# Up-projection products held in source order, with two grouped pairs at the start of each second half

## The chip, the cores and the metric

The kernel runs on one core of one Trainium2 chip. The metric is the device time of one execution in microseconds. The kernel before takes 2371.57 us (median of three runs, 2370.21 to 2375.67). Besides, one execution was taken by the hardware profiler; every time inside the kernel in this document is from that trace, in microseconds from the first instruction.

The engines have short names. PE is the matrix engine (its weight loads are listed apart, as PEld), DVE the vector engine, ACT the scalar engine, POOL the general one, and SP issues most of the transfers. A matrix product takes a stationary operand of 128 x 128 and streams up to 512 columns past it. Its results are added up in a bank of PSUM.

## The reference

The program is an encoder of two layers on 256 tokens of width 2048. Each layer has a normalisation, a token mixer (mLSTM in layer 0, HGRN2 in layer 1), a second normalisation, and a gated MLP with a convolution of width 3. The change touches the MLP alone:

```python
D_MODEL, SEQ, DEPTH, D_FF, CONV_W = 2048, 256, 2, 5504, 3

def conv_glu(hn, w_up, conv_w, conv_b, w_down):
    u = hn @ w_up
    a, v = jnp.split(u, 2, axis=-1)
    s = a.shape[1]
    pad = CONV_W // 2
    ap = jnp.pad(a, ((0, 0), (pad, pad), (0, 0)))
    c = conv_b
    for j in range(CONV_W):
        c = c + ap[:, j:j + s] * conv_w[j]
    return (jax.nn.gelu(c, approximate=False) * v) @ w_down

for layer in range(DEPTH):
    ...
    h = h + mix
    h = h + conv_glu(rmsnorm(h, norm_ffn_g[layer]), ffn_w_up[layer], ffn_conv_w[layer],
                     ffn_conv_b[layer], ffn_w_down[layer])
return rmsnorm(h, final_g)
```

Everything is float32. The kernel gets that precision out of products of a reduced kind of float32: each operand is split into a high part and a low part, and high x high, high x low and low x high are added up.

## The kernel before

**Chunks.** All products with weights are cut into chunks (`Chunk`, L124), which `stream` (L324) takes one after the other. A chunk of the kind "fm" has 256 weight columns. Its result is 2 x 128 columns by 256 tokens, in two banks of PSUM, one for each `f`. The chunk runs over `nk` = 16 slices of the input, called tiles here; a slice is 128 of the 2048 features. For every tile and each of the two `f` there are two products. The wide one (L356) has the high part of 128 weight columns stationary (`wh`) and streams 512 columns: the input's high part for 256 tokens and its low part for the same tokens. The narrow one (L360) has the low part stationary (`wl`) and streams the 256 columns of the input's high part. One wide and one narrow product are called a pair here; a chunk has 32 pairs.

**The order in the source.** For each piece of weights `stream` makes a list `ops` of (tile, f, part), with "h" for wide and "l" for narrow (L347). So the products come in turn: wide, narrow, wide, narrow. An entry `i` in `swap` exchanges the narrow product of pair `i` and the wide one of pair `i` + 1 (L348 to L351). This makes wide, wide, narrow, narrow out of these two pairs, and that is called a group here.

**The order on the chip** is not that of the source. The whole program is handed to a scheduler (L1363) that plays it through with estimated times. On each engine it issues, of what its plan has ready, what comes first in the source. Something the plan expects late is overtaken by what stands behind it. Afterwards the order on each engine is fixed, and at run time an engine waits where an input isn't there yet. `pin` (L130) is a call that ties an instruction behind the last one that the source has on the same engine, in issue order alone. It is used for the loads of weights that are `paced` (`late`, L393), and in the first chunk of all.

**The weights' way.** The loads (L394, L135) bring 2048 columns at a time into three buffers, `raw`. ACT makes the high part of 1024 columns (L147), and DVE subtracts it for the low part (L148). There are four buffers for each part, and a piece is made three pieces ahead of its use (`LOOK`). Four tiles of an up chunk fit one piece.

**The MLP** (`ffn`, L1174). The 5504 features are 43 chunks, each with 128 columns of `a` and 128 of `v`. They are done in two halves (L1215). The first half (`part` 0) has 22 up chunks (704 pairs) and then the products with `w_down` for these features. The second half (`part` 1) has 21 up chunks (672 pairs) and its `w_down` products. The latter are 512 columns wide throughout (L236, result `pc` or `mm`, stationary `g` or `sx`). Between the products of a first half's chunk 0, PE also has the transposes of the normalisation (L433) and the small products that spread its factors (L457). The slices of the input are made by ACT (L378) and DVE (L379) from these transposes, so the first chunk's last tiles need slices that are made while the chunk runs. `prepare` (L612) loads weights of the down stage early, combines them on DVE (L631) and stores them; `side.tick` counts products to pace such side work.

Up chunks come from L1226 to L1229. The only groups that the source before has in the MLP are one in the second chunk of each first half (`swap=(3,)`: the fourth and fifth pair) and one in the first chunk of each second half (`swap=(2,)`: the two pairs of the second tile). HGRN's "fm" chunks (L1157) have groups as well.

Of the kernel before, what the change touches and what calls it, by code (L numbers as in the profile page):

```python
# [15 lines left out]
P = 128  # L16
T = 256
# [49 lines left out]
def trunk_kernel(ctx, tc, xT, x_d, fg_d, pp_d, cst_d, w_gate, w_first, w_aq, w_ak, w_av, w_ao, w_aout, w_ao2,  # L67
                 w_bq, w_bv, w_bg, w_bout, w_bo2, w_up, w_d0, w_d1, w_d3, out, mscr, tscr):
    nc = tc.nc
    act, dve, pool, pe = nc.scalar, nc.vector, nc.gpsimd, nc.tensor  # L70
# [22 lines left out]
    class Side:  # L93
        def __init__(self):
            self.now, self.jobs = 0.0, []
# [26 lines left out]


    class Chunk:  # L124
        def __init__(self, kind, src, nk, x, done, before=None, last=False, swap=(), first=False, paced=False):
            self.last, self.swap, self.first, self.paced = last, swap, first, paced
            self.kind, self.src, self.nk, self.x, self.done, self.before = kind, src, nk, x, done, before
            self.width = {"fm": 256, "tm": 512, "st": 512}[kind]

    pin = tc.keep_in_program_order  # L130
# [91 lines left out]
    def banks():  # L222
        return [psm.tile([P, 512], F32, tag="mm", name="mm") for _ in range(2)]
# [100 lines left out]
    def stream(chunks):  # L324
        pieces = split_weights(chunks)
        ready = []

        def fetch():
            p = next(pieces, None)
            if p is not None:  # L330
                ready.append(p)

        for _ in range(LOOK):
            fetch()
        for ch in chunks:
            if ch.before:
                ch.before()
            if ch.kind == "st":
                squares_by_seven(ch, fetch, ready)
                continue  # L340
            ps = banks()
            k = 0
            while k < ch.nk:
                fetch()
                wh, wl, n = ready.pop(0)
                if ch.kind == "fm":
                    ops = [(kk, f, part) for kk in range(n) for f in range(2) for part in "hl"]  # L347
                    for i in ch.swap:  # L348
                        i -= 2 * k
                        if 0 <= i < 2 * n - 1:  # L350
                            ops[2 * i + 1:2 * i + 3] = ops[2 * i + 2], ops[2 * i + 1]  # L351
                    for kk, f, part in ops:
                        x = ch.x(k + kk)
                        c = kk * ch.width + f * P
                        if part == "h":
                            pe.matmul(ps[f], wh[:, c:c + P], x, start=k + kk == 0, stop=False)  # L356
                            continue
                        if f:
                            side.tick(0.65)
                        pe.matmul(ps[f][:, 0:T], wl[:, c:c + P], x[:, 0:T], start=False, stop=k + kk == ch.nk - 1)  # L360
                    k += n
                    continue
                for kk in range(n):
                    x = ch.x(k)
                    st, sp = k == 0, k == ch.nk - 1
                    c = slice(kk * 512, (kk + 1) * 512)
                    ops = [(t, i) for t in range(2) for i in range(3)]
                    if ch.first and k in (0, 2):
                        ops.sort(key=lambda o: (0, 2, 1)[o[1]])
                    for t, i in ops:  # L370
                        a, w = ((0, wh), (0, wl), (T, wh))[i]
                        pe.matmul(ps[t], x[:, a + t * P:a + (t + 1) * P], w[:, c], start=st and i == 0, stop=sp and i == 2)  # L372
                    side.tick(1.3)
                    k += 1
            ch.done(ps)
# [236 lines left out]
    def prepare(tiles, todo, first, period, finished, start, ahead):  # L612

        loaded = []

        def load(i):
            if i < len(todo):
                r = tiles(i)
                for j in range(2):
                    start(r[j], todo[i][0][:, j * 1024:(j + 1) * 1024])  # L620
                loaded.append(r)

        yield first
        load(0)
        for i, (_, dst) in enumerate(todo):
            yield period / 2
            if ahead:
                load(i + 1)
            B11, B22, B21, B12 = (loaded[i][j // 2][:, j % 2 * 512:(j % 2 + 1) * 512] for j in range(4))
            for x, y, out in ((B12, B22, B22), (B12, B11, B12), (B11, B22, B11), (B21, B11, B21)):  # L630
                dve.tensor_tensor(out, x, y, ALU.subtract)  # L631
                yield period / 24
            for j in range(2):
                nc.sync.dma_start(dst[:, j * 1024:(j + 1) * 1024], loaded[i][j])
            yield period / 3
            if not ahead:
                load(i + 1)
        finished.append(True)
# [8 lines left out]
    def store(ch, src, u, todo):  # L647
        ch.stored[u] = tscr[turns["t"]]
        turns["t"] += 1
        todo.append((src[:, 2048 * u:2048 * (u + 1)], ch.stored[u]))  # L650
# [523 lines left out]
    def ffn(layer, norm, nxt):  # L1174
# [5 lines left out]
        def begin():  # L1180
            box["mp"] = stack.enter_context(tc.tile_pool(name="ff", bufs=1))
            box["mp"].tile([P, LEAD], F32, name="lead")
            for ch in pairs:
                ch.pool = box["mp"]
            if ending:
                nxt.begin(box["mp"])
# [28 lines left out]
        for part, (f0, nf) in enumerate(((0, FA), (FA, FB))):  # L1215
            GT, SX, todo, finished = [], {}, [], []
            lists.append((todo, finished))

            def prep(todo=todo, finished=finished, nf=nf):
                if not pairs[0].pool:  # L1220
                    begin()
                side.push(prepare(lambda i: [box["mp"].tile([P, 1024], F32, tag=("wh", "wl")[i % 2], bufs=MORE, name="praw")
                                             for _ in range(2)],
                                  todo, 18.0, (nf * 10.4 - 26.0) / len(todo), finished, late, True))

            for i in range(nf):  # L1226
                chunks.append(Chunk("fm", w_up[layer, f0 + i], KT, norm.x, done_up(f0 + i, i, GT, SX, SEVEN[layer][part]),
                                    prep if i == 0 else None,
                                    swap=(2,) if part and i == 0 else (3,) if f0 + i == 1 else (), paced=True))  # L1229
            def two(src, c0, norm, seven, fly, shares, GT=GT, SX=SX, nf=nf):  # L1230
                ch = pair(src, nf, c0, lambda k: GT[k], lambda u: SX[u], norm, seven)
                ch.waits, left = [], [u for u in seven if u not in fly]
                for n, (todo, finished) in zip(shares, [early[layer]] + lists):
                    for u in left[:n]:
                        store(ch, src, u, todo)
                    if n:
                        ch.waits.append(finished)
                    left = left[n:]
                assert not left
                pairs.append(ch)  # L1240
                return ch

            w0, w1 = w_d0[layer][:, f0 * 1024:(f0 + nf) * 1024], w_d3[layer] if part else w_d1[layer]
            seven, fly = SEVEN[layer][part], FLY[2 * layer + part]
            n = len(seven) - len(fly)
            chunks.append(two(w0, 0, nxt if part else None, seven, fly, (0, 0, n) if part else (FIRST, n - FIRST)))
            chunks.append(two(w1, 2, nxt if part and not ending else None, seven, fly, SPLIT[layer] if part else (0, n)))
            if part:
                chunks[-1].last = ending
                if ending:  # L1250
                    chunks[-2].before, chunks[-1].half = nxt.load, nxt.half
                else:
                    chunks[-1].ends = True
# [12 lines left out]
    nf = FinalNorm()  # L1266
    chunks = mlstm(n0, n1)
    c, close0 = ffn(0, n1, n2)
    chunks += c
    c = hgrn(n2, n3)  # L1270
# [5 lines left out]
    c[0].before = swap  # L1276
    chunks += c
    c, close1 = ffn(1, n3, nf)
    chunks += c
    stream(chunks)  # L1280
    close1()

# [98 lines left out]
```

## Time and profile before

| | us |
|---|---|
| median of the runs | 2371.57 |
| profiled execution | 2370.59 |
| its span, first to last instruction | 2368.6 |
| layer 0, up products of the first half | 389.3 to 634.9 |
| layer 0, up products of the second half | 742.7 to 975.6 |
| HGRN mixer of layer 1 with its products | 1106.0 to 1560 |
| layer 1, up products of the first half | 1665.3 to 1910.8 |
| layer 1, up products of the second half | 2015.1 to 2255.6 |

The profile has one page for the whole execution, with the busy time of each engine, and views that are asked for a stretch, a line or an engine: the waits, the timeline, groups by line, and the busy time by stretches. In the timeline, products of the same group that follow each other directly stand in one row, with their count behind the x. The ends of matrix products are modelled, so two of them seem to overlap; what tells the pace is the distance from one start to the next. Operands are named without their number, so a row of L356 doesn't tell its tile or its chunk; these follow from counting.

### The profile page before, as it was taken

To read this page: it belongs to the slowest core of one execution; us is meant where nothing else is said; L and a number is where in the kernel's file an instruction comes from. 1 tells how busy PE (TensorE), PEld (TensorE's weight loads), DVE (VectorE), ACT (ScalarE), POOL (GpSimd) and SP (SyncE) were. 2 spreads that over 40 slices of the span, in tenths; PEclk is the share of its full clock that TensorE was granted. 3 is DMA by queue.
4 is the path that set the end of the run, shared out by engine and by line. 5 is a ranking of instruction groups with operands and counts; after the bars stand their busy time and mean duration, and the time that the engine had idled before them with its cause. 6 is when DMAs were issued, how large, how long until landed. Compare 5 with 4: busy or idle time off the path is not lost. (4 is left out here: it accounts for less than half of the span.)

```text
span 2368.6 us, 38410 instructions
## 1 busy us (share of the span) xinstructions
PE 2358.2 (100%) x14545; PEld 2018.0 (85%) x14545; DVE 1991.6 (84%) x3087; ACT 1469.8 (62%) x2340; POOL 196.7 (8%) x244
## 2 busy tenths in 40 slices
PE   9999999999999999999999999999999999999998
PEld 8888888888888888888888888888888888888887
DVE  7777687888998898897888888778788889888878
ACT  7655456555665555676777677766555566455565
POOL 0100000000000000000232322220000000000000
PEclk9999999999999999999999999999999999999999
DMA  8776656888889888996656665656788888888896
GB/s 302 238 246 244 213 195 208 298 281 295 307 322 331 303 286 294 323 333 231 211 201 226 205 229 198 212 178 221 267 299 301 292 326 324 294 285 292 310 349 221
DMA packets 122266, 632.97 MB, mean 267 GB/s; under 512 B 13776, under 2 KB 14928, under 8 KB 77664
## 3 DMA queue, kind: packets, MB, share of 16 engines
q1 hardware_dynamic: 120384, 626.51, 75.1%
q0 software_dynamic: 1120, 3.21, 0.8%
q8 instruction: 114, 1.87, 0.3%
q10 hardware_dynamic: 576, 0.79, 0.1%
q14 instruction: 72, 0.59, 0.1%
HBM read 562.24 MB, written 68.22 MB: 266 GB/s over the span
## 5 line engine op out<-in xcount | busy, mean ns | idle before, releaser
L356 PE MATMUL mm<-xt,wh 128*128 128x512 f32 x3776 | 1316.6, 395 | 0.0
L148 DVE TENSOR_TENSOR wl<-raw,wh 128x1024 fp32r<-128x1024 f32 (+1 forms) x844 | 1035.0, 1231 | 231.1 <-ACT wh L147 222.2
L147 ACT CAST wh<-raw 128x1024 fp32r<-128x1024 f32 (+1 forms) x844 | 875.7, 1043 | 530.0 <-PE mm L356 325.6
L360 PE MATMUL mm<-xt,wl 128*128 128x256 f32 x3776 | 1045.6, 279 | 0.0
L356 PEld LDWEIGHTS mm<-xt,wh 128*128 128x128 f32 x3776 | 705.7, 188 | 163.1 <-ACT jk L535 0.4
L360 PEld LDWEIGHTS mm<-xt,wl 128*128 128x128 f32 x3776 | 710.0, 188 | 4.8
L372 PE MATMUL mm<-wh,xt 128*128 128x512 f32 x1024 | 324.4, 392 | 1.3 <-ACT wh L147 1.2
L236 PE MATMUL pc<-wh,g 128*128 128x512 f32 (+1 forms) x716 | 243.1, 388 | 0.1
L372 PEld LDWEIGHTS mm<-wh,xt 128*128 128x128 f32 x1024 | 191.1, 188 | 40.8 <-ACT wh L147 1.8
L631 DVE TENSOR_TENSOR praw<-praw 128x512 f32<-128x512 f32 x252 | 174.1, 691 | 35.4 <-DMA praw<-in_w_d 22.3
L372 PE MATMUL mm<-wl,xt 128*128 128x512 f32 x512 | 199.7, 391 | 0.0
L236 PEld LDWEIGHTS pc<-wh,g 128*128 128x128 f32 x716 | 134.1, 188 | 28.4 <-ACT wh L147 0.9
L236 PE MATMUL mm<-wh,sx 128*128 128x512 f32 x432 | 153.4, 389 | 0.0
L148 DVE TENSOR_TENSOR wl<-T,wh 128x1024 fp32r<-128x1024 f32 (+1 forms) x144 | 136.0, 955 | 16.0 <-ACT wh L147 15.6
L147 ACT CAST wh<-T 128x1024 fp32r<-128x1024 f32 (+1 forms) x144 | 118.5, 834 | 48.4 <-DMA T<-tscr 21.7
L236 PE MATMUL pc<-wl,g 128*128 128x512 f32 (+1 forms) x358 | 138.9, 388 | 0.0
L590 POOL TENSOR_TENSOR hm<-hm,u 128x512 f32<-128x512 f32 x10 | 16.0, 1600 | 1222.4 <-DVE u L589 1170.7
L372 PEld LDWEIGHTS mm<-wl,xt 128*128 128x128 f32 x512 | 96.2, 188 | 18.6
L1194 ACT COPY avc<-mm 128x256 f32<-128x256 f32 x172 | 64.1, 373 | 75.5 <-PE mm L360 75.4
L1070 DVE TENSOR_TENSOR QK<-QK,G 128x256 f32<-128x256 f32 x224 | 104.3, 514 | 6.2 <-ACT kq L1049 5.9
L1049 ACT COPY kq<-QK 128x512 f32<-128x512 f32 x112 | 74.5, 669 | 36.9 <-DVE QK L1070 29.1
L236 PEld LDWEIGHTS mm<-wh,sx 128*128 128x128 f32 x432 | 81.0, 188 | 17.2 <-ACT wh L147 0.5
(246 smaller groups left out, 2259.9 us busy)
## 6 DMA issues: line engine op xcount, KB each, us to landing
raw<-in_w_up SPq DMA_DIRECT2D x172, 1024.0 KB, 6.0
tscr<-praw SPq DMA_DIRECT2D x126, 512.0 KB, 6.7
praw<-in_w_d SPq DMA_DIRECT2D x120, 512.0 KB, 6.7
raw<-in_w_bq SPq DMA_DIRECT2D x48, 1024.0 KB, 5.0
T<-tscr SPq DMA_DIRECT2D x63, 768.0 KB, 7.9
raw<-in_w_d SPq DMA_DIRECT2D x60, 768.0 KB, 6.4
raw<-in_w_ao SPq DMA_DIRECT2D x24, 1024.0 KB, 4.8
raw<-in_w_d SPq DMA_DIRECT2D x24, 1024.0 KB, 7.8
```

The source lines that it names most:

```text
L147: pin(act.copy(wh[:, :m], r))
L148: pin(dve.tensor_tensor(wl[:, :m], r, wh[:, :m].bitcast(F32), ALU.subtract))
L236: pin(pe.matmul(ps, a, b, start=bank not in begun, stop=stop and i == 2))
L356: pe.matmul(ps[f], wh[:, c:c + P], x, start=k + kk == 0, stop=False)
L360: pe.matmul(ps[f][:, 0:T], wl[:, c:c + P], x[:, 0:T], start=False, stop=k + kk == ch.nk - 1)
L372: pe.matmul(ps[t], x[:, a + t * P:a + (t + 1) * P], w[:, c], start=st and i == 0, stop=sp and i == 2)
L590: pool.tensor_tensor(part(1, 0), part(1, 0), u, ALU.add)
L631: dve.tensor_tensor(out, x, y, ALU.subtract)
L1049: act.copy(m, blocks(QK, h))
L1070: dve.tensor_tensor(two[:, j], two[:, j], by[:, j], ALU.mult)
L1194: act.copy(z, p[:, T:2 * T])
```

## The change

Chunks get a flag, `fixed`. The products of a chunk that has it are pinned, each behind what the source has before it on PE. All up chunks have the flag, but for the first chunk of each first half. The group list of the first chunk of each second half goes from `(2,)` to `(0, 2)`: a group on each of the first two tiles.

```diff
-        def __init__(self, kind, src, nk, x, done, before=None, last=False, swap=(), first=False, paced=False):
-            self.last, self.swap, self.first, self.paced = last, swap, first, paced
+        def __init__(self, kind, src, nk, x, done, before=None, last=False, swap=(), first=False, paced=False, fixed=False):
+            self.last, self.swap, self.first, self.paced, self.fixed = last, swap, first, paced, fixed
...
+                    hold = pin if ch.fixed else lambda ins: ins
                     for kk, f, part in ops:
                         x = ch.x(k + kk)
                         c = kk * ch.width + f * P
                         if part == "h":
-                            pe.matmul(ps[f], wh[:, c:c + P], x, start=k + kk == 0, stop=False)
+                            hold(pe.matmul(ps[f], wh[:, c:c + P], x, start=k + kk == 0, stop=False))
                             continue
                         if f:
                             side.tick(0.65)
-                        pe.matmul(ps[f][:, 0:T], wl[:, c:c + P], x[:, 0:T], start=False, stop=k + kk == ch.nk - 1)
+                        hold(pe.matmul(ps[f][:, 0:T], wl[:, c:c + P], x[:, 0:T], start=False, stop=k + kk == ch.nk - 1))
...
                 chunks.append(Chunk("fm", w_up[layer, f0 + i], KT, norm.x, done_up(f0 + i, i, GT, SX, SEVEN[layer][part]),
                                     prep if i == 0 else None,
-                                    swap=(2,) if part and i == 0 else (3,) if f0 + i == 1 else (), paced=True))
+                                    swap=(0, 2) if part and i == 0 else (3,) if f0 + i == 1 else (), paced=True,
+                                    fixed=part + i > 0))
```

## The prediction

> **What bounds the kernel now.** I read the page first, for the share of each engine, and then the view of waits for TensorE (PE): waited-for line, releaser, us in total, times, longest.
>
> ```profile
> span 2368.6 us, 38410 instructions
> ...
> PE 2358.2 (100%) x14545; PEld 2018.0 (85%) x14545; DVE 1991.6 (84%) x3087; ACT 1469.8 (62%) x2340; POOL 196.7 (8%) x244
> ```
>
> ```profile
> PE mm L372 <- ACT wh L147: 1.2, 2, 0.9
> PE idle L1264 <- POOL ones L1257: 1.1, 1, 1.1
> ```
>
> PE is busy for the whole span and waits 2.3 us in all. No engine, load or queue can give time back here; what is left is the pace at which PE takes its products. So the next view is that of stretches, asked for the wide up products alone (line 356). Its columns are the stretch, its length, PE's busy time with the number of products, the same for weight loads, granted clock, DMA share and GB/s. Each up product pair is one wide (512 columns, L356) and one narrow (256 columns, L360), so length over count is the time of one pair.
>
> ```profile
> 398.70:401.87 3.17, 3.17 (x9) 1.68 (x10) 1.00 0.83 253
> 403.60:634.80 231.20, 231.18 (x667) 124.97 (x667) 1.00 0.86 298
> 742.70:975.60 232.90, 232.76 (x672) 125.72 (x671) 1.00 0.86 301
> 1679.60:1910.80 231.20, 231.20 (x667) 124.94 (x667) 1.00 0.85 297
> 2024.50:2255.60 231.10, 231.08 (x654) 122.79 (x654) 1.00 0.87 301
> ```
>
> The same pair has two paces. It takes 231.20/667 = 346.6 ns in both first halves, 232.90/672 = 346.6 in layer 0's second half, and 231.10/654 = 353.4 in layer 1's second half; the short stretch at 398.70 has 3.17/9 = 352. The granted clock is 1.00 in all of them, and PE has no gap in any. The timeline of PE (start, time, line, operation, count) shows where layer 1's second half changes pace:
>
> ```profile
> 2023.72 0.27 PE L360 MATMUL mm<-xt,wl 128*128 128x256 f32 x1
> 2023.83 0.63 PE L356 MATMUL mm<-xt,wh 128*128 128x512 f32 x2
> 2024.29 0.40 PE L360 MATMUL mm<-xt,wl 128*128 128x256 f32 x2
> 2024.52 0.40 PE L356 MATMUL mm<-xt,wh 128*128 128x512 f32 x1
> ```
>
> At 2023.83 the scheduler put two wide products ahead of two narrow ones (a group, below), where the source has them in turn. Ahead of it the pairs run fast, behind it slow, to the end of the stage. The HGRN stage, where the source puts such groups on purpose, lets one see what a group does:
>
> ```profile
> 1111.22:1118.64 7.42, 7.42 (x21) 3.94 (x22) 1.00 0.71 222
> 1119.35:1129.73 10.38, 10.38 (x30) 5.61 (x31) 1.00 0.83 301
> 1130.44:1141.02 10.58, 10.58 (x30) 5.61 (x31) 1.00 0.59 201
> 1141.74:1150.73 8.99, 8.99 (x26) 4.75 (x26) 1.00 0.44 140
> ...
> 1268.11:1278.33 10.22, 10.22 (x29) 5.42 (x30) 1.00 0.69 235
> 1279.04:1288.23 9.19, 9.19 (x26) 4.77 (x26) 1.00 0.58 196
> ```
>
> Between each two consecutive rows lies one group and nothing else. The first four run 353, 346, 353, 346 ns a pair: each group turns the pace over. The last two run 352 and 353: a group that did not turn a slow stretch. The difference I can see is the number of slow pairs ahead of the group: 21 and 30 are multiples of three, 29 leaves two. Pair starts in slow stretches repeat every third pair, which fits. I take as the working rule: a group in a fast stretch makes it slow; a group in a slow one makes it fast, unless the slow pairs ahead of it leave two when divided by three.
>
> **The change, part by part.** *The pins* (`hold`) add edges in issue order alone: no instruction, transfer or semaphore. They cost nothing by themselves; what they change is the order in which PE gets its products, in every up chunk but the first of each first half, and, through the scheduler's planned times, possibly the order elsewhere. There are three places where the order before departs from the source.
>
> (1) *Layer 1, second half, ninth tile* (the group at 2023.83). It goes, so the 654 pairs behind it stay at the pace they had. At 353.4 - 346.6 = 6.7 ns each (6.73 before rounding) that is 654 x 6.73 = 4.4 us, all of it on PE and so on the end. For this the start has to be fast, which brings in the swap.
>
> (2) *Starts of the second halves.* The source before has its only group on the second tile; the source after has one on each of the first two. PE's timeline of layer 0 has both already, put there by the scheduler:
>
> ```profile
> 742.67 0.62 PE L356 MATMUL mm<-xt,wh 128*128 128x512 f32 x2
> 743.12 0.40 PE L360 MATMUL mm<-xt,wl 128*128 128x256 f32 x2
> 743.35 0.63 PE L356 MATMUL mm<-xt,wh 128*128 128x512 f32 x2
> 743.82 0.39 PE L360 MATMUL mm<-xt,wl 128*128 128x256 f32 x2
> ```
>
> So layer 0's start stays as it is, at a cost of 0, and its 672 pairs are fast. In layer 1 the first group was torn apart (timeline of PE, with two DVE rows set among them in order of time):
>
> ```profile
> 2011.61 1.22 DVE L148 TENSOR_TENSOR wl<-raw,wh 128x1024 fp32r<-128x1024 f32 x1
> ...
> 2013.94 2.35 DVE L148 TENSOR_TENSOR wl<-raw,wh 128x1024 fp32r<-128x1024 f32 x2
> 2013.98 1.29 PE L236 MATMUL pc<-wh,g 128*128 128x512 f32 x5
> 2015.11 0.62 PE L356 MATMUL mm<-xt,wh 128*128 128x512 f32 x2
> 2015.57 0.39 PE L236 MATMUL pc<-wl,g 128*128 128x512 f32 x1
> ...
> 2018.74 0.40 PE L360 MATMUL mm<-xt,wl 128*128 128x256 f32 x2
> ```
>
> Two wide up products went ahead of the last 14 products of the down stage. The pins put them behind, so the product of 2015.57 would start at 2015.11, 0.46 us sooner, and everything behind it on PE hangs on it. If its low half is the subtraction of 2011.61, done at 2012.83, it waits for nothing. If it is the first of the two from 2013.94, done at about 2015.12, and a weight load goes out some 0.23 us (one wide product) ahead, the stall is about 0.25 us. The bounds are 0 and 0.3; I take 0: a subtraction makes the low half of four tiles of an up chunk, the up chunk needs its first one at 2018.74 and its second eight pairs later, and the two from 2013.94 are in time for just these, so the earlier one is likely the down stage's last. After that, layer 1 starts as layer 0 does.
>
> (3) *First halves, where chunk 0 meets chunk 1.*
>
> ```profile
> 398.11 0.48 DVE L379 SCALAR_TENSOR_TENSOR xt<-pz,pp,xt 128x256 fp32r<-128x256 f32 x1
> ...
> 401.87 0.63 PE L356 MATMUL mm<-xt,wh 128*128 128x512 f32 x2
> 402.34 0.28 PE L360 MATMUL mm<-xt,wl 128*128 128x256 f32 x1
> 402.46 0.39 PE L356 MATMUL mm<-xt,wh 128*128 128x512 f32 x1
> 402.68 0.40 PE L360 MATMUL mm<-xt,wl 128*128 128x256 f32 x2
> 402.92 0.63 PE L356 MATMUL mm<-xt,wh 128*128 128x512 f32 x2
> ```
>
> Chunk 1's first five products stand ahead of chunk 0's last tile, which needs the last slice of the input: the scheduler expected it late. The timeline of DVE has it done at 398.11 + 0.48 = 398.59, and in source order it is needed five products earlier, near 401.2: 2.6 us of cover. If that cover were gone, PE would stand still and with it all behind it, by at most the 0.7 us that the five products took. I take 0. Then the pairs run W N in turn from 398.70 (slow) to chunk 1's group on its fourth and fifth pairs: the 9 of the row above and three more, 12, a multiple of three. By the working rule the group turns slow into fast, as it did behind 21 and 30, and the 667 pairs behind it stay fast. Three slow pairs and a group in place of the five pairs from 401.87 to 403.62 (1.75 us): 3 x 353 ns, and 0.70 us for a group (742.67 to 743.35 is 0.68, 2023.83 to 2024.52 is 0.69), 1.76 us. Cost 0.01 us. Layer 1 has the same rows 1276 us later.
>
> (4) *Order elsewhere.* The scheduler works through planned times, so a planned wait of PE in chunk 1 can shift what follows. The stage with much to move is HGRN, with its small products between the pairs. Groups by line, for the stretches of layer 0's second half, layer 1's second half and HGRN (count, busy, mean ns):
>
> ```profile
> L356 PE MATMUL mm<-xt,wh 128*128 128x512 f32 x667 | 231.3, 394 | 0.0
> ```
>
> ```profile
> L356 PE MATMUL mm<-xt,wh 128*128 128x512 f32 x653 | 230.8, 399 | 0.0
> ```
>
> ```profile
> L356 PE MATMUL mm<-xt,wh 128*128 128x512 f32 x768 | 268.6, 396 | 0.0
> ```
>
> A fast wide product is 394 ns, a slow one 399; HGRN's mean of 396 makes about 0.4 of its 768 pairs slow, some 300, worth 300 x 6.73 = 2.0 us. Bounds of a new order there: -2.0 (all fast) to +3.1 (the other 468 slow too). I take 0, since the planned order depends on what is ready relative to PE, and a shift of all engines leaves that alone.
>
> *Cover.* A faster layer 1 needs DVE and the loads to keep up (all engines in the stretch: PE, PEld, DVE, ACT, POOL, clock, DMA share, GB/s):
>
> ```profile
> 403.60:634.80 231.20, 231.20 (x1336) 202.19 (x1335) 203.73 (x332) 132.46 (x208) 0.00 (x0) 1.00 0.86 298
> 2024.50:2255.60 231.10, 231.10 (x1310) 200.40 (x1309) 197.18 (x313) 125.76 (x197) 2.21 (x4) 1.00 0.87 301
> ```
>
> DVE would have 197.2 us of work in 226.7 (0.87), where the first half already runs at 203.7 in 231.2 (0.88) without a wait of PE; the loads would go from 301 to 307 GB/s.
>
> **Sum**, against the profiled execution's own 2370.59 (its span of 2368.6 and 2.0 around it): -4.40 + 0.02 + 0 + 0 gives 2366.2. The median of the runs, 2371.57, lies 1.0 above that execution, so for a median I forecast 2367.2.
>
> **The rivals.**
> *A. No gain, 2371.6.* The pace does not hang on the order, or layer 1's second half falls back to slow elsewhere: 0 in place of -4.4. For it: I have the turning point from one stage and one place outside it. Against: every long stretch changes pace at a group or a break and nowhere else. The Trainium skill, page "TensorE: Matmul & The Clock Gate", section "Back-to-back issue gap", speaks for it: its gap for a product by itself follows from the columns alone, 518 and 262 cycles at 2.4 GHz, an estimate of 325 ns a pair in any order, by which the sum would be 2371.6. The trace disagrees, with 346.6 and 353.4 for the same pair. Chance 0.10.
> *B. Slower, 2376.2.* The group in chunk 1 fails to turn the slow stretch, as behind the 29 pairs at 1268. Place: first halves; price 667 x 6.73 = 4.5 us each; it decides as soon as the slow pairs ahead of the group leave two by three, or the rule is not what I think. Both halves: 2371.6 + 9.0 - 4.4 = 2376.2; one alone is +0.1, 2371.7. For it: the order there is new, and the rule rests on few stretches. Against: 12 is a multiple of three, and layer 0 is the same up to that place. Chance 0.08 for both, 0.04 for one.
> *C. HGRN is dealt anew:* 2367.2 - 2.0 to + 3.1, 2365.2 to 2370.3. Chance 0.10.
>
> **How the numbers follow.** The forecast has 0.68. Over 0.2% faster (about what a measurement of this kernel can tell from no change) means under 2366.8, 0.4 us below the forecast; the three runs shown lie from 1.4 below to 4.1 above their median. So I halve 0.68, and C likewise, and add a little for medians that fall low: faster 0.40. Within 0.2%: the other half of both, A, and B in one half of a layer: 0.52. Slower: B in both, 0.08. The range reaches down to C's best with the runs' spread, 2364.0, and up past A by 1.0, 2372.6; only B in both lies outside.
>
> **What would show it.** Right: the stretch of layer 1's second half at 346.6 ns a pair from its second group on, about 4.4 us shorter; 14 more products ahead of its first wide one; no group at its ninth tile; W and N in turn where chunk 0 meets chunk 1, then 667 pairs at 346.6; HGRN's W mean still 396. Wrong: 399 for W in a first half (B), in layer 1's second half (A), or waits of PE above the 2.3 us.

## The result, and the profile after

The kernel after takes 2366.59 us (median of nine runs, 2364.73 to 2369.58) where the kernel before takes 2371.57 in nine runs beside it. The ratio is 0.998, with an interval of 0.9971 to 0.9989, so it is faster, by 2.6 to 6.9 us or about 0.2%. The profiled execution took 2366.48 (before: 2370.59). The page and the view of waits for PE, as read before:

```profile
span 2364.5 us, 38407 instructions
...
PE 2354.1 (100%) x14545; PEld 2016.2 (85%) x14545; DVE 1993.5 (84%) x3087; ACT 1470.0 (62%) x2340; POOL 196.5 (8%) x244
```

```profile
PE idle L1266 <- POOL ones L1259: 1.1, 1, 1.1
PE mm L236 <- DVE wl L148: 0.5, 1, 0.5
PE mm L373 <- ACT wh L147: 0.5, 2, 0.3
PE pc L236 <- ACT wh L147: 0.2, 1, 0.2
```

PE has the same 14545 products, still fills the span and still waits 2.3 us in all. What went is 4.1 us of its busy time. The lines of the up products moved by one, so that the wide product is L357 and the narrow one L361. The view of stretches for the wide products after:

```profile
398.12:402.36 4.24, 4.24 (x12) 2.25 (x13) 1.00 0.85 295
403.05:634.25 231.20, 231.19 (x667) 124.96 (x667) 1.00 0.86 299
742.15:975.05 232.90, 232.75 (x672) 125.75 (x671) 1.00 0.85 301
1678.05:1909.27 231.22, 231.18 (x667) 124.99 (x667) 1.00 0.85 297
2017.37:2250.27 232.90, 232.76 (x672) 125.75 (x671) 1.00 0.86 302
```

All four long stretches now run at 232.90/672 = 346.6 or 231.2/667 = 346.7 ns a pair, at a granted clock of 1.00 as before. The first row is the 12 slow pairs ahead of chunk 1's group, 4.24/12 = 353 ns. The next two extracts are from PE's timeline: first where layer 0's chunk 0 meets chunk 1, then the start of layer 1's second half.

```profile
402.01 0.40 PE L357 MATMUL mm<-xt,wh 128*128 128x512 f32 x1
402.25 0.28 PE L361 MATMUL mm<-xt,wl 128*128 128x256 f32 x1
402.36 0.63 PE L357 MATMUL mm<-xt,wh 128*128 128x512 f32 x2
402.83 0.39 PE L361 MATMUL mm<-xt,wl 128*128 128x256 f32 x2
403.06 0.40 PE L357 MATMUL mm<-xt,wh 128*128 128x512 f32 x1
```

```profile
2014.20 0.39 PE L236 MATMUL pc<-wl,g 128*128 128x512 f32 x1
...
2017.14 0.39 PE L236 MATMUL pc<-wh,g 128*128 128x512 f32 x1
2017.37 0.61 PE L357 MATMUL mm<-xt,wh 128*128 128x512 f32 x2
2017.83 0.40 PE L361 MATMUL mm<-xt,wl 128*128 128x256 f32 x2
2018.06 0.63 PE L357 MATMUL mm<-xt,wh 128*128 128x512 f32 x2
2018.53 0.39 PE L361 MATMUL mm<-xt,wl 128*128 128x256 f32 x2
```

The torn group is gone. The 14 down products from 2014.20 stand ahead of the up products, 3.17/14 = 226 ns each, with no gap. Behind 2018.53 come 668 pairs in turn, without the group that the ninth tile had.

To see where the 4.1 us lie, one asks for the wide line stage by stage: count, least, median and longest duration in ns, and first and last start. For the kernel before these are layer 0's second half, HGRN, and layer 1's first and second halves:

```profile
L356 PE MATMUL mm<-xt,wh x672: 389/394/397, 742.7 to 975.3; 128*128 128x512 f32 x168
...
L356 PE MATMUL mm<-xt,wh x768: 387/395/499, 1106.0 to 1548.4; 128*128 128x512 f32 x192
...
L356 PE MATMUL mm<-xt,wh x704: 387/395/475, 1665.3 to 1910.5; 128*128 128x512 f32 x176
...
L356 PE MATMUL mm<-xt,wh x672: 389/398/403, 2015.1 to 2255.3; 128*128 128x512 f32 x168
```

The same for the kernel after:

```profile
L357 PE MATMUL mm<-xt,wh x672: 389/394/397, 742.2 to 974.8; 128*128 128x512 f32 x168
...
L357 PE MATMUL mm<-xt,wh x768: 387/395/496, 1105.0 to 1546.9; 128*128 128x512 f32 x192
...
L357 PE MATMUL mm<-xt,wh x704: 389/395/475, 1663.7 to 1909.0; 128*128 128x512 f32 x176
...
L357 PE MATMUL mm<-xt,wh x672: 389/394/397, 2017.4 to 2250.0; 128*128 128x512 f32 x168
```

| part of the span, us | before | after | difference |
|---|---|---|---|
| up to layer 0's second half | 742.7 | 742.2 | -0.5 |
| from there to HGRN's first up product | 363.3 | 362.8 | -0.5 |
| HGRN, first to last up product | 442.4 | 441.9 | -0.5 |
| from there to the last up product of layer 1's first half | 362.1 | 362.1 | 0.0 |
| its down products, with the 14 that moved | 107.8 | 108.4 | +0.6 |
| layer 1's second half, without the 14 | 237.0 | 232.6 | -4.4 |
| from there to the end | 113.3 | 114.5 | +1.2 |
| span | 2368.6 | 2364.5 | -4.1 |

For the down products and the second half of before, 14 x 0.2266 = 3.2 us were moved from one row to the other. The median of the row that was to change, 398 ns a wide product before, is 394 now. The rest adds up to +0.3. Its largest term, +1.2, holds the 0.5 that PE waited for DVE's subtraction (L148). The order in this last part is the same in the profiles of before, after, e1, e2 and e4 to e7, on PE, DVE and ACT. These experiments take between 114.0 (e4) and 117.1 us (e5, 2366.1 - 2249.0) for it, so with one and the same order it differs between executions by more than 1.2.

### The profile page after: what moved, and what is told of

Its sections match the earlier page's. It is cut to its first block, busy times and chain, and to the rows that moved or that the text cites. A ratio compares the mean times of both kernels' runs of the same rounds, so it can differ in the third digit from the quotient of the medians.

```text
span 2364.5 us, 38407 instructions
## 1 busy us (share of the span) xinstructions
PE 2354.1 (100%) x14545; PEld 2016.2 (85%) x14545; DVE 1993.5 (84%) x3087; ACT 1470.0 (62%) x2340; POOL 196.5 (8%) x244
## 5 line engine op out<-in xcount | busy, mean ns | idle before, releaser
L357 PE MATMUL mm<-xt,wh 128*128 128x512 f32 x3776 | 1312.0, 394 | 0.0
L148 DVE TENSOR_TENSOR wl<-raw,wh 128x1024 fp32r<-128x1024 f32 (+1 forms) x844 | 1037.3, 1234 | 222.6 <-ACT wh L147 214.5
L361 PE MATMUL mm<-xt,wl 128*128 128x256 f32 x3776 | 1043.5, 278 | 0.0
L357 PEld LDWEIGHTS mm<-xt,wh 128*128 128x128 f32 x3776 | 705.6, 188 | 160.6 <-issue 0.4
L361 PEld LDWEIGHTS mm<-xt,wl 128*128 128x128 f32 x3776 | 709.4, 188 | 4.5
L148 DVE TENSOR_TENSOR wl<-T,wh 128x1024 fp32r<-128x1024 f32 (+1 forms) x144 | 135.9, 955 | 13.3 <-ACT wh L147 8.9
```

What stands on the lines that cost most here:

```text
L148: pin(dve.tensor_tensor(wl[:, :m], r, wh[:, :m].bitcast(F32), ALU.subtract))
L357: hold(pe.matmul(ps[f], wh[:, c:c + P], x, start=k + kk == 0, stop=False))
L361: hold(pe.matmul(ps[f][:, 0:T], wl[:, c:c + P], x[:, 0:T], start=False, stop=k + kk == ch.nk - 1))
```

## The experiments

My theory ahead of the runs: the pace of the pairs hangs on the order alone. A group in a fast stretch makes it slow; a group in a slow one makes it fast, unless the slow pairs ahead leave two by three. The rivals: the gain comes from something else that the pins do, and the pace falls as it does by chance; or the pace is the cost of each change between wide and narrow products. All edits are against the kernel after, in the line of the up chunks if nothing else is said. Each time is a median beside runs of the kernel before on the same chip (2371.03 for e1, e2, e4 and e6; 2371.30 for e5, e7, e8 and e9; 2371.46 for e10 and e11).

### e1: the group put back

```diff
-swap=(0, 2) if part and i == 0 else (3,) if f0 + i == 1 else ()
+swap=((0, 2, 16) if layer else (0, 2)) if part and i == 0 else (3,) if f0 + i == 1 else ()
```

> The changed kernel with one group put back by hand, held, at the 17th and 18th pair of layer 1's second half; PE's order differs from the changed kernel in these two products alone, and all other engines' orders are those of the changed kernel. Theory (the gain is the pace of the pairs behind that group): the 654 pairs behind it run at 353.4 ns in place of 346.7, 4.4 us more than the changed kernel, so a ratio of about 1.000 to the kernel before (2371). Rival (the gain is from the new order of ACT, DVE and loads where chunk 0 meets chunk 1, or from the down products put back in order): that stays, ratio 0.998 (2366.6).

Measured: 2371.66 us, ratio to before 1.0002 (0.9993 to 1.001). The order on PE differs from after in two products only. Stretches of the wide products ahead of the group and behind it:

```profile
2021.27:2025.42 4.15, 4.15 (x12) 2.24 (x13) 1.00 0.20 85
2026.12:2257.20 231.08, 231.07 (x654) 122.78 (x654) 1.00 0.87 301
```

346 ns a pair ahead and 231.08/654 = 353.3 behind. One exchange of two products takes the whole gain back. The pins stood, and so did the order on ACT, DVE and POOL, so the gain isn't something else that they do.

### e2: the pins alone

```diff
-swap=(0, 2) if part and i == 0 else ...
+swap=(2,) if part and i == 0 else ...
```

> The pins without the second group: each second half starts with two pairs in turn and then the one group of the second tile. Theory (pace by group; two pairs and a group made the mLSTM chunks fast each time): both second halves at 346.7 ns a pair, ratio 0.998 to the kernel before. Rival (it takes groups on both tiles to start fast): 668 pairs slow in both layers, 668 x 6.7 = 4.5 us each, 9.0 us over the changed kernel, ratio about 1.002 (2375.6).

Measured: 2367.81 us, ratio 0.9988 (0.998 to 0.9997). Both second halves are fast; layer 1's, in the view of stretches and at its start in PE's timeline:

```profile
2018.74:2251.66 232.92, 232.85 (x672) 125.75 (x671) 1.00 0.87 301
```

```profile
2018.72 0.39 PE L357 MATMUL mm<-xt,wh 128*128 128x512 f32 x1
...
2019.41 0.64 PE L357 MATMUL mm<-xt,wh 128*128 128x512 f32 x2
...
2020.13 0.40 PE L357 MATMUL mm<-xt,wh 128*128 128x512 f32 x1
```

With a single group, at 2019.41, the stage takes 232.92 us, as with two. So the pins carry the gain and the second group isn't needed. The other part of the change alone was not run: without the pins the scheduler, given `(0, 2)`, arrives at the order of before on every engine, so there is nothing to time.

### e4, e5 and e6: fewer slow pairs ahead of the group, and no group

In e4 and e5 the group in the second chunk of the first halves stands earlier, behind 11 or 10 slow pairs in place of 12; in e6 the second halves have no group.

```diff
-... else (3,) if f0 + i == 1 else ()
+... else (2,) if f0 + i == 1 else ()      # e4
+... else (1,) if f0 + i == 1 else ()      # e5
-swap=(0, 2) if part and i == 0 else (3,) if f0 + i == 1 else ()
+swap=(3,) if f0 + i == 1 else ()          # e6
```

> The changed kernel with chunk 1's group in the first halves one pair sooner: 11 slow pairs ahead of it since the last break, in place of 12. Theory (a group turns a slow stretch unless the pairs ahead leave two when divided by three; 11 does): both first halves stay slow, 668 x 6.7 = 4.5 us each, 9.0 us over the changed kernel, ratio about 1.002 (2375.6). Rival (every group turns the pace over, whatever the count): first halves at 346.7 ns, ratio 0.998 (2366.6).

> The changed kernel with chunk 1's group in the first halves two pairs sooner: 10 slow pairs ahead of it, which leaves one by three. Theory (only a remainder of two fails to turn): first halves at 346.7 ns, span as the changed kernel's, 2364.5. Rival (it takes a multiple of three): both stay slow, 669 x 6.7 = 4.5 us each, span about 2373.5.

> The changed kernel without any group in the second halves: wide and narrow in turn from the first pair. Theory (pairs in turn start slow behind wide products, and only a group makes them fast): 672 pairs at 353.4 ns in both second halves, 2 x 4.5 = 9.0 us over the changed kernel, ratio about 1.002 (2375.6). Rival (a stretch is fast unless something disturbs it, the groups at the start do nothing): ratio 0.998 (2366.6).

Measured: e4 2376.91 us, ratio 1.0023 (1.0013 to 1.0033); e5 2368.06 in one run; e6 2374.55, ratio 1.0019 (1.001 to 1.0028). The stretches behind the group in e4's two first halves:

```profile
404.69:640.72 236.03, 236.02 (x668) 125.41 (x668) 1.00 0.86 295
1684.87:1920.90 236.03, 236.02 (x668) 125.41 (x668) 1.00 0.85 292
```

In e5, layer 0:

```profile
401.98:633.92 231.94, 231.93 (x669) 125.34 (x669) 1.00 0.87 299
```

In e6, layer 1's second half:

```profile
2026.37:2263.79 237.42, 237.42 (x672) 126.08 (x671) 1.00 0.86 296
```

Behind 11 pairs, which leave two by three, the group doesn't turn the pace: 236.03/668 = 353.3. Behind 10 it does (231.94/669 = 346.7), and behind 12, in the kernel after. One pair more or less ahead of one group decides over 667 pairs, in both layers alike. The kind of group isn't what decides: e4's takes both pairs of one tile, where those of e5 and after reach over two tiles, but HGRN's groups behind 21 and 30 slow pairs also take both pairs of one tile, and they turn. e4 is 10.3 us above after, of which 2 x 668 x 6.7 ns = 9.0 lie in these two stretches. Without a group the pairs start slow and stay slow, 237.42/672 = 353.3, which is 2 x (237.42 - 232.90) = 9.0 us on both second halves; the median is 8.0 above that of after. PE's timeline shows that the slow pace isn't even: in e6 the wide products from 742.58 on start at 742.93, 743.29, 743.64, 743.99 and 744.35, so that every third distance is 0.36 us and the others 0.35.

### e7: fewer groups in HGRN

If a group costs the pace, HGRN with its many groups should gain from having fewer.

```diff
-swap=(2, 13) if n in TMS else (4, 15)
+swap=(2,) if n in TMS else ()
```

> The changed kernel with fewer groups in HGRN: one on the second tile of each first chunk behind a wide stretch, none elsewhere (two or one per chunk before); only PE's order differs. Theory (each further group turns a fast stretch slow): HGRN's stretches stay fast until small products break in, so of some 300 slow pairs most go, 1 to 2 us: ratio to the kernel before 0.9975 (2365), mean of the wide product in HGRN 395 or below in place of 396. Rival (the small products between the pairs set HGRN's pace, not the groups): nothing moves, ratio 0.998.

Measured: 2368.09 us, ratio 0.9986 (0.9977 to 0.9995), no better than after: the gain that the theory expected did not come, and the mean of the wide product stayed at 396. Three of its HGRN stretches, wide products alone, and then the group of the wide products for the whole stage (count, busy, mean ns):

```profile
1107.18:1150.19 43.01, 43.00 (x124) 23.15 (x124) 1.00 0.68 225
1267.52:1287.68 20.16, 20.15 (x57) 10.61 (x57) 1.00 0.57 194
1331.87:1356.27 24.40, 24.39 (x69) 12.96 (x69) 1.00 0.69 247
```

```profile
L357 PE MATMUL mm<-xt,wh 128*128 128x512 f32 x768 | 270.3, 396 | 0.0
```

The first 124 pairs came out fast throughout (43.01/124 = 346.8), as groups that turn the pace would have it. But behind other products between the pairs the pace is slow again, and with no group to turn it back it stays so for 57 and 69 pairs (353.7 and 353.6). The wide products take 270.3 us, after 268.1 in the kernel after. Here the groups also bring slow stretches back to the fast pace.

### e8 and e9: groups throughout, and blocks of four

If each change between a wide and a narrow product cost something, groups throughout would halve the changes, and blocks of four wide and four narrow products halve them again. The edits are shortened:

```diff
+swap=tuple(range(0, 2 * KT, 2)) if part else (3,) if f0 + i == 1 else ()     # e8
+ops = [o for a in range(0, len(ops), 8) for p in "hl" for o in ops[a:a + 8] if o[2] == p]   # e9, second halves, without swap
```

> The changed kernel with groups throughout the second halves: two wide, two narrow, for all 1344 pairs. Theory (the pace is a state that a group disturbs; a group behind other pairs took 0.69 to 0.70 us before): 345 to 350 ns a pair, -2 to +4.4 us on the changed kernel, ratio to the kernel before 0.997 to 1.000. Rival (what costs is each change between wide and narrow; groups halve them, down to the 226.6 + 113 ns that wide behind wide and narrow behind narrow take): 340 ns, 1344 x 6.7 = 9.0 us less than the changed kernel, ratio 0.994 (2357.6).

> The changed kernel with four wide products ahead of four narrow ones throughout the second halves. Theory (pace as a state): as with groups of two throughout, 345 to 350 ns a pair, ratio 0.997 to 1.000. Rival (each change between wide and narrow costs): at or below the run with groups of two, 340 ns a pair or less, ratio 0.994 or below.

Measured: e8 2369.90 us, ratio 0.9994 (0.9985 to 1.0004); e9 2372.76, ratio 1.0007 (0.9998 to 1.0016). Layer 1's second half in e8 by stretches:

```profile
2020.80:2254.90 234.10, 211.03 (x672) 102.17 (x671) 1.00 0.87 301
```

The same in e9, where the wide product is L360:

```profile
2021.90:2257.70 235.80, 183.41 (x672) 114.72 (x671) 1.00 0.86 301
```

And a piece of PE's timeline in e9:

```profile
800.46 1.09 PE L360 MATMUL mm<-xt,wh 128*128 128x512 f32 x4
801.39 0.63 PE L364 MATMUL mm<-xt,wl 128*128 128x256 f32 x4
801.86 1.09 PE L360 MATMUL mm<-xt,wh 128*128 128x512 f32 x4
```

A pair takes 234.10/672 = 348.4 ns in e8 and 235.80/672 = 350.9 in e9 (1.40 us for four, 800.46 to 801.86). Both lie between the two paces, e9's 0.9 above the 350 that the theory allowed. Fewer changes are not faster, so a cost that each change adds by itself falls as the cause.

### e10 and e11: 32 columns more

A candidate for the cause is the weight load: a wide product behind a wide one starts after 226 ns, so a narrow one of half the columns has about 113 to stream (an estimate), while one weight load takes 125.75/671 = 187 ns by the row of the stretches above. A narrow product of 288 columns covers more of the next load. Both kernels let the narrow products of the second halves also stream the first 32 columns of the input's low part, which adds a piece of low x low to the output of those columns. e10 has no group in the second halves, e11 the groups of after.

```diff
-pe.matmul(ps[f][:, 0:T], wl[:, c:c + P], x[:, 0:T], ...)
+pe.matmul(ps[f][:, 0:ch.cols], wl[:, c:c + P], x[:, 0:ch.cols], ...)    # cols = T + 32 * part
-swap=(0, 2) if part and i == 0 else (3,) if f0 + i == 1 else ()
+swap=(3,) if f0 + i == 1 else ()                                        # e10 alone
```

> The run without groups in the second halves, with the narrow products there 288 columns wide in place of 256: they also take the first 32 columns of the input's low part, a small term that is left out otherwise. The 32 columns are 13.3 ns of streaming (512 more columns in the wide product than none go with 226.6 ns and 256 with about 113, so some 0.44 ns a column). Theory (the slow pace comes of the weight load for the wide product, which is made behind the short narrow product and doesn't quite fit): with 13 ns more room the pairs run at the fast pace plus 13.3, 360 ns, in any order. Rival (the two paces have nothing to do with the narrow product's length): slow plus 13.3, 366.7 ns. Over 1344 pairs that is a span of about 2382 by the theory and 2391 by the rival.

> The changed kernel (groups on the first two tiles of the second halves) with the same 288 columns. Both theories: fast plus 13.3, 360 ns a pair, span about 2382. Beside the run without groups: equal by the theory, 9 us shorter by the rival.

Measured, in one run each: 2388.11 and 2388.65 us. Layer 0's second half by stretches (wide product L358) in e10:

```profile
741.96:986.11 244.15, 244.15 (x672) 125.95 (x671) 1.00 0.84 287
```

In e11:

```profile
742.20:986.20 244.00, 243.80 (x672) 125.83 (x671) 1.00 0.84 287
```

244.15/672 = 363.3 and 244.00/672 = 363.1 ns: with 288 columns there is one pace whether there is a group or not. That is what the weight load would do as the cause; but the 32 columns cost 16.6 ns over the fast pace and 10.0 over the slow one, where 32 x 226.6/512 = 14.2 would be their streaming (an estimate; the 13.3 of the expectation doesn't follow from its own 0.44 ns a column). Neither the 360 of the theory nor the 366.7 of the rival came. The weight load is not shown as the cause, and the two paces' mechanism stays open.

## Why the prediction was right, step by step

**What bounds the kernel.** PE's pace, with waits of 2.3 us before and after: right.

**Term 1, the group at the ninth tile, -4.40.** The stage went from 237.0 to 232.6, -4.4. e1 shows the cause by the reverse, with 353.3 ns behind the group put back. The +0.6 and +1.2 in the down stages are not its price as far as the profiles tell: in e1, where the stage is slow again, the last part still takes 114.3 us, against 114.5 in the kernel after and 113.3 before; and the 108.4 of the down products of layer 1's first half is 107.8 or 107.9 in e1, e2 and e4 to e7.

**Term 2, the starts, 0 with a stall of at most 0.3.** No stall: the 14 down products ran at 226 ns each into the first up product. But the reason for the swap, "the start has to be fast, which brings in the swap", was too much said. By e2 one group on the second tile, the source's old one, does as well. And that group has two pairs ahead of it (0.69 us, 345 ns each), where the rule leaves the stage slow whichever pace they are given: a group in a fast stretch makes it slow, and one behind two slow pairs doesn't turn them. Nor does the rule fit two groups at a start that is slow without one (e6): the second would turn the stage back, and in the kernel after it doesn't. So the count by three holds for the slow stretches in which it was read and tested (21, 30, 10, 12 turn, 29 and 11 do not), but not from every start. What it counts from is open.

The other half of the rule, that a group in a fast stretch makes it slow, holds at 2023.83 (12 fast pairs ahead) and behind HGRN's 30, but the profile of before already had a place in HGRN where it fails, with 21 fast pairs, a group at 1415.92, and 26 more at 9.01/26 = 347 ns:

```profile
1408.62:1415.92 7.30, 7.28 (x21) 3.94 (x22) 1.00 0.76 274
1416.62:1425.63 9.01, 9.00 (x26) 4.77 (x26) 1.00 0.53 176
```

Terms 1 and 3 rest on what a group does at their own places, and there it came as forecast.

**Term 3, the first halves, +0.01 each.** The order came as worked out: 12 slow pairs, the group, 667 fast pairs, and no wait of PE for the last slice of the input. In layer 0 it is 236.10 us from 398.70 to the end of the half before, and 236.13 from 398.12 after. e4 and e5 show that the remainder mattered. Rival B was the right danger: in e4 both first halves fail, and its 2376.91 stands beside the 2376.2 that B priced, 9.0 above before for the two halves less 4.4 in layer 1's second.

**Term 4, order elsewhere, 0.** The order in HGRN is the same, product for product. Yet its stage is 0.5 us shorter, because some stretches changed pace with no change of order in this stage. The two at 1268 and 1279, slow in the profile of before, stand in the profile of after as

```profile
1267.15:1277.21 10.06, 10.06 (x29) 5.42 (x30) 1.00 0.69 233
1277.92:1286.93 9.01, 9.01 (x26) 4.76 (x26) 1.00 0.53 176
```

with 347 and 347 ns a pair in place of 352 and 353, on both sides of a group that thus turned nothing, in a fast stretch this time. It went the other way too: the 30 pairs at 1341 took 10.40 us before and 10.60 after. So that the pace hangs on the order alone is shown for the long up stretches, and not for HGRN. The reason given ("a shift of all engines leaves that alone") was right for the order, not for the pace: rival C does not need a new order. Its size here is a quarter of the 2.0 us that bounded it.

**The sum.** The profiled execution was forecast at 2366.2 and took 2366.48; the median at 2367.2 and came at 2366.59. The difference of the profiled execution to the median was not the 1.0 that I carried over from before, but 0.1. That the total came within 0.3 us is in part luck: the term of -4.4 is as forecast, but the other rows of the table moved by up to 1.2 us each and cancel to +0.3. It is luck too that the median fell just beyond the 0.2% of the prediction's chances, at 2366.59 where 2366.8 was the line.

**Rival A** fell with the stage itself. The rule of the Trainium skill that spoke for it (page "TensorE: Matmul & The Clock Gate", section "Back-to-back issue gap"), by which the columns alone give the gap of a product by itself, does not carry over to these pairs: the same columns gave 346.6, 348.4, 350.9 and 353.3 ns with nothing changed but the order.

## What to carry to other kernels

When one engine fills the span and never waits, look at its pace stretch by stretch: length over count, at equal granted clock, and then at the first instruction where it changes. A pattern of products that runs at two paces can be decided by a handful of products near its start, so fix their order by hand where a scheduler is free to move them, and try a few places for such an exchange, since one pair more or less decides. Where other products stand among the pattern, as in HGRN here, neither the order of the pairs nor fewer exchanges give the pace for certain.

## What the runs showed of the hardware that was not expected

- The pace of pairs can differ between two executions (here one of each kernel) with the same order on PE in that stage (HGRN at 1268: 352 before, 347 after), by 0.5 us over the stage.
- Two wide and two narrow products in groups throughout take 348.4 ns a pair, blocks of four 350.9. A wide product behind a wide one takes 226, and with half of it for a narrow one a pair would be 340 (an estimate); no order tried came nearer than 346.6.
- With 32 columns more in the narrow product the difference between the two orders is gone, at 363 ns a pair (one run of each).
